# Fused passes over t on DVE, one-hots from a distance, and two gathers in one run

## The chip, the cores and the metric

One core of a Trainium2 chip runs the whole program. The metric is the device time of one execution in microseconds, the median of several runs. TensorE (PE) multiplies, VectorE (DVE) and GpSimd (Pool) work elementwise, ScalarE (ACT) applies functions and copies, SyncE (SP) issues the weight loads. Profiles name the five engines by these short names.

## The reference, cut to what matters

The program computes one step of a two-layer network on 384 tokens (128 context, 256 latent) of width 1024. Each layer is a token mixer and then a mixture of experts:

```
x = layer_norm(ALPHA * x + g1 * mix, ln1_g, ln1_b)          # r is the sum, normalised later
t = x * (1 + sc2) + sh2                                      # what the experts see
group  = argmax(t @ rg_w + rg_b)                             # 1 of 4 groups
top_v, top_i = top_k(t @ re_w + re_b  within the group, 2)   # 2 of its 8 experts
gate   = softmax(top_v) * softmax(group logits)[group]
y      = sum over the two experts e of gate_e * (silu(t @ w1_e) * (t @ w3_e)) @ w2_e
x = layer_norm(ALPHA * x + g2 * y, ln2_g, ln2_b)
```

The reference multiplies every token with all 32 experts and weights by the gate. The kernel computes only the two experts of each token: it sorts the 768 pairs (token, expert) by expert, gathers the rows of t in that order, and runs the experts on windows of 32 rows.

## The kernel before, in words

Tokens lie in NT = 3 tiles of 128. The last column block of the output projection and everything up to the routing is in `last_col` (L983). Per tile i it multiplies (`prod`), adds the residual and takes statistics (`ln1_part`, `ln1_tile`; the reciprocal root is made by Pool, L115 and L116), and transposes r for the logits. `t` of a tile is made in two passes over 1024 columns, `(r - mean) * gain` and `* rstd + bias`. Tile 0 has both fused on DVE (L1022, L1030). Tiles 1 and 2 are normalised by ACT and then multiplied and shifted by Pool (L1003, L1006), tile 2's shift by DVE. For products at nearly full precision t is split in two rounded parts, `thi` (ACT) and `tlo` = t - thi (L1012).

`route` (L1098) masks the expert logits of other groups, takes the two largest, makes one-hot rows `E` of the expert numbers, and counts with matmuls against a triangle of ones how many pairs lie before each (`pc`, a PSUM bank). From that follows `pos`, for each token the two places of its pairs among 768. Three one-hot matrices per block J of 256 places (`onehot`, L1287) are made by DVE with two comparisons of the row numbers 0..255 against the two places of a token, the second adding to the first. A gather is then 48 matmuls of 256 columns: for 8 blocks of 128 rows of t, 3 tiles and the parts thi and tlo, `t^T @ onehot`. `gather0` (L1336) takes tile after tile into four banks; `gather(1)` and `gather(2)` (L1321) take bank after bank, two tags with two buffers each, and each needs its one-hots, which have three buffers. The evacuations write `xT`, transposed rows in expert order.

`second` (L1167) works out which experts have more than CAP = 32 rows and the registers `who`, `more` and `first`; `gates` the softmaxes; `slots` (L1227) builds one-hots of ranks (`RO`) and values (`V`) and multiplies them (12 matmuls, L1252) into the destinations and gates of each row. `windows(q)` copies six windows of 32 rows of xT for quad q by register. `up` (L1377) multiplies a window with quarter kq of the weights of a quad of four experts; `copies` (L1366) copies the weights of experts with an additional window; `down` multiplies with w2, and `scatter` writes the rows to `y_d` in device memory. A weight tile is 1 MB; `done` frees one and lets SP load a later one.

Order: inside `manual_schedule` the engines named there keep the order of the text. In `last_col` that holds for DVE, Pool, ACT and PE, in `experts` before the change for PE alone; DVE, ACT and Pool are ordered there by a planner that simulates the engines, and it may also put instructions of later code into gaps of an ordered part. `issue_after` adds one dependency. The pool `lp` of `last_col` is closed before `experts`, and the pool `ep` (xT, hv, ys) lies over its memory; a tile waits until the tiles under it are no longer used. PSUM has eight banks: tags tp, sc, mm and ms, two each.

Of the kernel before, what the change touches and what calls it, by code (L numbers as in the profile page):

```python
# [8 lines left out]
F32 = mybir.dt.float32  # L9
# [11 lines left out]
D = 1024  # L21
# [56 lines left out]
class Kern:  # L78
# [795 lines left out]
    def open_ln1(self, l):  # L874
# [5 lines left out]
        self.mo = self.ohp = P("mo", bufs=1)  # L880
# [102 lines left out]
    def last_col(self, l, w0, w1):  # L983
# [12 lines left out]
        def norm(i):  # L996
            self.act(t[i], self.r[:, i, :], AF.Identity, scale=self.rs1[:, i:i + 1], bias=self.nm1[:, i:i + 1])

        def nmul(i):
            G.tensor_tensor(self.nm1[:, i:i + 1], self.nmean[:, i:i + 1], self.rs1[:, i:i + 1], op=ALU.mult)  # L1000

        def gain(eng, i, z=slice(0, D)):
            eng.tensor_tensor(t[i][:, z], t[i][:, z], rows["sc20"][:, z], op=ALU.mult)  # L1003

        def bias(eng, i, z=slice(0, D)):
            eng.tensor_tensor(t[i][:, z], t[i][:, z], rows["sh20"][:, z], op=ALU.add)  # L1006

        def hi(i, z=slice(0, D)):
            self.act(self.thi[:, i, z], t[i][:, z], AF.Copy)

        def lo(eng, i, z=slice(0, D)):
            eng.tensor_tensor(self.tlo[:, i, z], t[i][:, z], self.thi[:, i, z].bitcast(F32), op=ALU.subtract)  # L1012

        with self.tc.manual_schedule(engines={e.engine for e in (V, G, nc.scalar, nc.tensor)}):
# [7 lines left out]
            V.scalar_tensor_tensor(t[0], self.r[:, 0, :], self.nmean[:, 0:1], rows["sc21"], op0=ALU.add, op1=ALU.mult)  # L1022
            prod(1, 1)
            self.logit_mm(3, 0)
            self.ln1_part(l, 3, ts, 1)
            self.ln1_tile(l, 1)
            nmul(1)
            prod(2, 0)
            self.logit_tr(3, 1, ts)
            V.scalar_tensor_tensor(t[0], t[0], self.rs1[:, 0:1], rows["sh21"], op0=ALU.mult, op1=ALU.add)  # L1030
            t[1] = lp()
            norm(1)
            gain(G, 1, slice(0, 512))
# [21 lines left out]
            nmul(2)  # L1055
            gain(G, 1, slice(512, D))
# [11 lines left out]
            for z in (slice(0, 512), slice(512, D)):  # L1068
                bias(V, 2, z)
                hi(2, z)  # L1070
            for z in (slice(0, 512), slice(512, D)):
                lo(V, 2, z)
            for i in range(NT):
                G.dma_start(self.t_d[i * 128:(i + 1) * 128, :], t[i])

# [22 lines left out]
    def route(self, l, el):  # L1098
# [40 lines left out]
        self.warm(3)  # L1139
        pr = lpt("pr", (NT, 2, NE))  # L1140
# [4 lines left out]
        self.pos_ins = nc.vector.tensor_reduce(pos.rearrange("p i c -> p (i c)"), pr.rearrange("p i c e -> p (i c) e"), axis=AX.X, op=ALU.add)  # L1145
        self.pc, self.m8, self.e8 = pc, m8, e8

# [19 lines left out]
    def second(self):  # L1167
# [4 lines left out]
        self.posj = S("posj", (2, N6))  # L1172
        for J in range(2):
            V.tensor_scalar(self.posj[:, J, :], pos, -256.0 * (J + 1), None, op0=ALU.add)
        cnt = self.pc[:, 96:128].rearrange("p (q e) -> p q e", e=4)
# [14 lines left out]
        V.tensor_copy(tb[:, 1], self.pc[:, 128:160])  # L1190
# [27 lines left out]
        self.first = S("first", (NE,), I32)  # L1218
        V.tensor_copy(self.first, tb[:, 1])
# [67 lines left out]
    def onehot(self, J):  # L1287

        nc = self.nc
        iota = self.con[:, C_I256:C_I256 + 256]  # L1290
        sj = self.posj[:, J - 1, :] if J else self.place.rearrange("p i c -> p (i c)")
        out = []
        for i in range(NT):
            oh = self.ohp.tile([128, 256], F32R, tag="oh", name="oh", bufs=3)
            nc.vector.tensor_scalar(oh, iota, sj[:, 2 * i:2 * i + 1], None, op0=ALU.is_equal)
            self.oh_ins = nc.vector.scalar_tensor_tensor(oh, iota, sj[:, 2 * i + 1:2 * i + 2], oh.bitcast(F32),
                                                         op0=ALU.is_equal, op1=ALU.add)
            out.append(oh)
        if J == 0:
            self.oh0_ins = self.oh_ins  # L1300
        return out


    def experts(self, l):
# [16 lines left out]
        def gather(J):  # L1321

            oh = self.onehot(J)
            for z in range(4):
                ps = self.bank(("tp", "sc")[z % 2])
                for d2 in range(2):
                    d = z * 2 + d2
                    n = 0
                    for i in range(NT):
                        for t in (self.thi, self.tlo):  # L1330
                            nc.tensor.matmul(ps[:, d2 * 256:(d2 + 1) * 256], t[:, i, d * 128:(d + 1) * 128], oh[i],
                                             start=n == 0, stop=n == 5)
                            n += 1
                evac(J, z, ps)

        def gather0(oh):  # L1336

            ps = [self.bank(("tp", "sc")[z % 2]) for z in range(4)]
# [5 lines left out]
            for n, (i, t) in enumerate(((0, self.thi), (1, self.thi), (0, self.tlo), (1, self.tlo))):  # L1344
                mm(i, t, range(8), n == 0, False)
# [566 lines left out]
```

## Time and profile before

| | us |
|---|---|
| median of 3 runs | 1156.14 (1154.74 to 1159.78) |
| the profiled execution | 1157.68 |
| its span | 1155.8 |
| PE busy | 1026.5 (89%) |
| DVE busy | 822.6 (71%) |
| ACT busy | 414.1 (36%) |
| Pool busy | 288.5 (25%) |
| HBM traffic | 248 GB/s over the span |

The span runs from the first to the last instruction of the profiled execution. A row of a timeline gives the start, the duration, the engine, the line, the operation, the tile written and read, the shape and, in brackets, how long the engine was idle before it and what released it. Consecutive instructions of one kind stand in one row with their count. A line number such as L100 can be that of a helper (L100 is every ACT operation).

### The profile page before, as it was taken

The numbers are of one execution on the slowest core, as the hardware profiler recorded it, in microseconds if no ns is written. First come the engines' busy times: TensorE is split into PE (matmuls) and PEld (weight loads), VectorE is DVE, ScalarE is ACT, GpSimd is POOL, SyncE is SP. The second block draws the span as 40 slices with busy tenths as digits, with TensorE's granted clock in tenths as the row PEclk, the third lists the DMA queues.
The fourth block names the chain that finished last, engine by engine and source line by source line (L and its number), as shares of the span: only waits on it lengthen the run. The fifth ranks groups of instructions, "written<-read, shape, count | busy, mean of one in ns | idle before, by whom it ended". The sixth has DMA issues, their size and how long they took to land. (4 is left out here: it accounts for less than half of the span.)

```text
span 1155.8 us, 20809 instructions
## 1 busy us (share of the span) xinstructions
PE 1026.5 (89%) x8182; PEld 849.1 (73%) x8182; DVE 822.6 (71%) x1530; ACT 414.1 (36%) x739; POOL 288.5 (25%) x246
## 2 busy tenths in 40 slices
PE   7999999999999867966779999999999996887764
PEld 5898968878999856532349897788899996853322
DVE  4389999964457785752479999997744687766338
ACT  4334344443334123422253433444523432233222
POOL 0002411321100550323244043124020055013235
PEclk9999999999999887987989999999999999789787
DMA  9967578357357460999685756764234575279965
GB/s 355 413 241 270 216 253 314 122 184 273 128 203 267 177 237 23 400 420 415 239 346 192 282 202 244 261 254 153 73 112 143 219 274 228 83 273 420 419 260 197
DMA packets 55101, 282.73 MB, mean 245 GB/s; under 512 B 8060, under 2 KB 12284, under 8 KB 27857
## 3 DMA queue, kind: packets, MB, share of 16 engines
q1 hardware_dynamic: 49632, 269.99, 61.2%
q0 software_dynamic: 5360, 11.29, 2.5%
q8 instruction: 69, 1.13, 0.4%
q14 instruction: 40, 0.32, 0.1%
HBM read 262.11 MB, written 24.71 MB: 248 GB/s over the span
## 5 line engine op out<-in xcount | busy, mean ns | idle before, releaser
L95 PE MATMUL ps_mm<-hThi,wr 128*128 128x384 f32 x672 | 229.7, 343 | 5.0 <-ACT hThi L100 2.5
L96 PE MATMUL ps_mm<-hTlo,wr 128*128 128x384 f32 x672 | 227.9, 339 | 0.5 <-DVE hTlo L439 0.4
L108 DVE TENSOR_TENSOR wr<-w_raw,wr 128x1024 fp32r<-128x1024 f32 x124 | 161.8, 1305 | 93.5 <-ACT wr L100 93.3
L97 PE MATMUL ps_mm<-hThi,wr 128*128 128x384 f32 x672 | 227.8, 339 | 0.0
L503 DVE SCALAR_TENSOR_TENSOR cacc<-pad,par,cacc 128x399 f32<-128x399 f32 x240 | 170.1, 709 | 4.2
L100 ACT ACTIVATE wr<-w_raw 128x1024 fp32r<-128x1024 f32 x140 | 147.4, 1055 | 67.4 <-PE ps_mm L97 36.6
L95 PEld LDWEIGHTS ps_mm<-hThi,wr 128*128 128x128 f32 x672 | 127.0, 189 | 19.9 <-ACT hThi L100 4.9
L96 PEld LDWEIGHTS ps_mm<-hTlo,wr 128*128 128x128 f32 x672 | 127.1, 189 | 4.9 <-DVE hTlo L439 2.3
L97 PEld LDWEIGHTS ps_mm<-hThi,wr 128*128 128x128 f32 x672 | 127.2, 189 | 1.8 <-issue 1.0
L1431 POOL DMA_INDIRECT y_d<-ys,dst x28 | 28.6, 1022 | 195.0 <-DVE ys L1446 84.5
L108 POOL TENSOR_TENSOR wr<-w_raw,wr 128x1024 fp32r<-128x1024 f32 x10 | 24.3, 2433 | 200.6 <-ACT wr L100 200.2
L1419 PE MATMUL ps_sc<-w,hidT 128*32 128x512 f32 x256 | 42.6, 750 | 35.7 <-ACT ys L100 24.7
L1389 PE MATMUL ps_mm<-hv,win 128*32 128x128 f32 x1024 | 45.4, 285 | 6.7 <-DVE hv L1374 6.5
L1389 PEld LDWEIGHTS ps_mm<-hv,win 128*32 128x32 f32 x1024 | 33.4, 116 | 24.3 <-DVE hv L1374 13.8
L1383 PE MATMUL ps_mm<-w_raw,win 128*32 128x256 f32 x640 | 50.6, 438 | 0.0
L1374 DVE COPY hv<-w_raw 128x512 f32 x60 | 36.5, 644 | 19.6 <-PE ps_mm L1389 12.0
L100 ACT ACTIVATE gate<-ps_mm 128x384 f32<-128x384 f32 x40 | 19.6, 491 | 84.7 <-PE ps_mm L97 83.6
L217 PE MATMUL ps_ms<-w_raw,cT 128*32 128x512 f32 x320 | 47.7, 624 | 0.0
L1419 PEld LDWEIGHTS ps_sc<-w,hidT 128*32 128x32 f32 x256 | 8.2, 121 | 52.9 <-ACT ys L100 36.8
L909 POOL TENSOR_TENSOR rtmp<-sc,lb 128x1024 f32<-128x1024 f32 x4 | 9.9, 2491 | 122.2 <-DMA lb<-in_ln 122.2
L840 POOL TENSOR_TENSOR merged<-merged,gate 128x384 f32<-128x384 f32 x16 | 18.1, 1138 | 84.8 <-DVE gate L839 84.8
L100 ACT ACTIVATE win<-xT 128x256 f32 x64 | 21.5, 410 | 49.0 <-PE ps_mm L1383 47.6
(497 smaller groups left out, 2450.0 us busy)
## 6 DMA issues: line engine op xcount, KB each, us to landing
w_raw<-in_wst SPq DMA_DIRECT2D x68, 1024.0 KB, 6.3
w_raw<-in_wada SPq DMA_DIRECT2D x48, 1024.0 KB, 5.1
w_raw<-in_w SPq DMA_DIRECT2D x40, 1024.0 KB, 9.7
w<-in_w SPq DMA_DIRECT2D x32, 1024.0 KB, 18.9
w_x<-in_w SPq DMA_DIRECT2D x24, 1024.0 KB, 16.6
bias<-in_bias SPq DMA_DIRECT2D x8, 768.0 KB, 7.4
y_d<-zero SPq DMA_DIRECT2D x2, 3072.0 KB, 14.6
yy<-y_d SPq DMA_DIRECT2D x6, 1024.0 KB, 7.0
```

Source lines behind the costliest of these rows:

```text
L95: mm(out, whi, xhi, start=first, stop=False)
L96: mm(out, whi, xlo, start=False, stop=False)
L97: mm(out, wlo, xhi, start=False, stop=last)
L100: return self.nc.scalar.activation(out, in_, f, **k)
L108: (eng or self.nc.vector).tensor_tensor(lo, x, hi.bitcast(F32), op=ALU.subtract)
L217: nc.tensor.matmul(ps[32 * t:32 * t + 32, :], self.cT[:, 2 * kp + k, :], w[:, t * 512:t * 512 + 512], start=(kp == 0 and k == 0), stop=(kp ...
L503: nc.vector.scalar_tensor_tensor(acc, pad[:, j:j + W], w, acc, op0=ALU.mult, op1=ALU.add)
L1374: nc.vector.tensor_copy(hv[:, i, :], src)
L1383: nc.tensor.matmul(ps[e * 32:(e + 1) * 32, 0:256], x[:, k, e * 32:(e + 1) * 32], w[:, e, kk, :], start=k == 0, stop=k == 7, skip_group_che ...
L1389: nc.tensor.matmul(ps[t * 32:(t + 1) * 32, 256:384], x[:, k, 128 + i * 32:160 + i * 32], hv[:, i, kk, h * 128:(h + 1) * 128], start=False, ...
L1419: nc.tensor.matmul(po[e * 32:(e + 1) * 32, :], hT[:, e * 32:(e + 1) * 32], w2[:, e, :], start=True, stop=True)
L1431: ins = nc.gpsimd.indirect_dma_start(out=view, out_offset=bass.IndirectOffsetOnAxis(ap=dst, axis=0), in_=rows, in_offset=None, bounds_chec ...
```

## The change

In `last_col` the helpers for Pool and ACT go; `mean(i)` and `bias(i)` do both passes on DVE for all three tiles, each one fused instruction. The helper's order of the text changes with it: bias(0) stands ahead of the second tile's residual, mean(1) behind the second tile's statistics, bias(1) inside `route` behind the counting matmuls, mean(2) and bias(2) behind the one-hots of tiles 0 and 1. The gather's matmuls of blocks J = 0 and J = 1 move into `last_col` and run tile by tile, part by part, into eight banks. `route` also works out for each token `mid` = -(p0 + p1) - 512 * (-J), and `dist` = |p0 - p1|; a one-hot is then |2 * iota + mid| (ACT, AF.Abs) compared with dist (DVE). The counts are copied out of `pc` early. In `experts` the rest of the start is written in a fixed order for DVE, ACT and PE: one-hots of block 2, evacuation 0, the registers `first`, `second`, evacuation 1, gather 2, evacuation 2, the other registers, the first windows. `gates` waits for the last window copy, and `slots` stands behind the four products of quad 0.

```diff
-            nmul(1)
+            t[1] = lp()
+            mean(1)
...
-            hi(0)
             t[2] = rows["g11"]
-            norm(2)
-            bias(G, 1)
-            hi(1)
-            lo(G, 0)
-            gain(G, 2)
+            self.thilo(0, t, hi=True)
             self.warm(4)
-            self.route(l, self.logit[:, :, 8:40])
-            self.oh0 = self.onehot(0)
-            lo(V, 1)
...
+            self.route(l, self.logit[:, :, 8:40], lambda: bias(1))
+            hots(0)
+            self.counts()
+            hots(1)
+            self.thilo(1, t, hi)
+            self.gps = {}
+            for i in range(2):
+                self.gather_mm(oh, (0, 1), i, hi)
+            self.thilo(0, t, lo)
+            self.thilo(1, t, lo)
+            for i in range(2):
+                self.gather_mm(oh, (0, 1), i, lo)
+            mean(2)
+            bias(2)
+            hots(2)
+            self.thilo(2, t, hi)
+            self.thilo(2, t, lo)
             for i in range(NT):
                 G.dma_start(self.t_d[i * 128:(i + 1) * 128, :], t[i])
+            for part in (hi, lo):
+                self.gather_mm(oh, (0, 1), 2, part)
...
+    def gather_mm(self, oh, Js, i, part):
+        t = self.thi if part else self.tlo
+        first, last = (i, part) == (0, True), (i, part) == (2, False)
+        for J in Js:
+            for d in range(8):
+                if first and d % 2 == 0:
+                    self.gps[J, d // 2] = self.bank((("tp", "sc"), ("mm", "ms"))[J % 2][d // 2 % 2])
+                self.nc.tensor.matmul(self.gps[J, d // 2][:, d % 2 * 256:(d % 2 + 1) * 256], t[:, i, d * 128:(d + 1) * 128], oh[J, i],
+                                      start=first and d % 2 == 0, stop=last and d % 2 == 1, skip_group_check=True)
...
+        self.act(far, iota, AF.Abs, scale=2.0, bias=self.mid[:, J, i:i + 1])
+        self.nc.vector.tensor_scalar(oh, far, self.dist[:, i:i + 1], None, op0=ALU.is_equal)
...
-        with tc.manual_schedule(engines={nc.tensor.engine}):
-            gather0(self.oh0)
-            with tc.issue_after(self.oh0_ins.ins):
-                self.second()
-            gather(1)
-            gather(2)
+        with tc.manual_schedule(engines={e.engine for e in (nc.vector, nc.scalar, nc.tensor)}):
+            for i in range(NT):
+                self.onehot(oh[2, i], far[:, i, :], 2, i)
+            evacs(0)
+            first = regs(self.first[0:1], [nc.scalar.engine], 2 * T, ...)
+            self.second()
+            evacs(1)
+            for i in range(NT):
+                for part in (True, False):
+                    self.gather_mm(oh, (2,), i, part)
+            evacs(2)
...
+            x = windows(0)
+        with tc.manual_schedule(engines={nc.tensor.engine}):
+            with tc.issue_after(self.win_ins.ins):
+                self.gates(self.logit)
...
+                if q == 0:
+                    self.slots()
```

## Rows read from the trace of the kernel before

**Rows 1.** The page, part 2: GB/s in 40 equal slices.

```profile
GB/s 355 413 241 270 216 253 314 122 184 273 128 203 267 177 237 23 400 420 415 239 346 192 282 202 244 261 254 153 73 112 143 219 274 228 83 273 420 419 260 197
```

**Rows 2.** Stages: us, busy PE, PEld, DVE, ACT, POOL, PEclk, DMA share, GB/s.

```profile
443.00:452.00 9.00, 7.66 (x48) 7.35 (x48) 4.17 (x14) 2.60 (x5) 0.00 (x0) 0.81 0.01 2
452.00:457.50 5.50, 2.77 (x16) 2.68 (x20) 1.99 (x10) 2.79 (x9) 0.00 (x0) 0.75 0.00 0
...
470.00:490.00 20.00, 18.66 (x350) 10.69 (x346) 17.07 (x29) 8.65 (x20) 9.16 (x6) 1.00 1.01 413
```

**Rows 3.** The same table, the weight stream of layer 0.

```profile
462.00:553.00 91.00, 71.09 (x1139) 37.01 (x1132) 46.92 (x93) 28.45 (x62) 28.95 (x20) 0.85 1.01 410
```

**Rows 4.** Timeline of SP's queue: the first load of the stage.

```profile
459.44 8.04 SPq L330 DMA_DIRECT2D w_raw<-in_w  x6
```

**Rows 5.** Timeline of PE, layer 0, gathers to first expert product.

```profile
425.31 0.99 PE L1341 MATMUL ps_tp<-oh,thi 128*128 128x256 f32 x2
...
426.52 0.63 PE L1341 MATMUL ps_tp<-oh,thi 128*128 128x256 f32 x2
426.95 0.63 PE L1341 MATMUL ps_sc<-oh,thi 128*128 128x256 f32 x2
...
428.13 0.40 PE L1341 MATMUL ps_sc<-oh,thi 128*128 128x256 f32 x2
428.37 0.40 PE L1341 MATMUL ps_tp<-oh,tlo 128*128 128x256 f32 x2
...
451.06 0.28 PE L1331 MATMUL ps_sc<-oh,tlo 128*128 128x256 f32 x1
...
457.44 1.94 PE L1383 MATMUL ps_mm<-w_raw,win 128*32 128x256 f32 x16
```

**Rows 6.** Timeline of DVE, layer 0, from the first tile's mean to the windows.

```profile
403.59 1.28 DVE L1022 SCALAR_TENSOR_TENSOR t<-r,nmean,sc 128x1024 f32<-128x1024 f32 x1
405.79 0.42 DVE L944 TENSOR_TENSOR r<-ps_tp,g 128x256 f32<-128x256 f32 x1 [0.91 <-PE ps_tp L488]
...
411.18 1.17 DVE L1089 SCALAR_TENSOR_TENSOR logits<-logits,rs,S 128x40 f32<-128x40 f32 x2
...
413.74 0.77 DVE L1153 TENSOR_TENSOR ex<-logits,m 128x12 f32<-128x12 f32 x1
...
414.62 2.39 DVE L1110 SCALAR_TENSOR_TENSOR em<-pen,logits 128x96 f32<-128x96 f32 x1
...
417.83 1.41 DVE L1154 TENSOR_TENSOR ex<-e 128x6 f32<-128x6 f32 x1
...
419.54 2.28 DVE L1122 TENSOR_TENSOR Eb<-E 128x96 bf16<-128x96 f32 x1
...
422.12 0.26 DVE L1127 TENSOR_TENSOR Eb<-below 128x96 bf16<-128x96 f32 x1
423.16 0.36 DVE L1141 TENSOR_TENSOR pr<-ps_ms,E 128x192 f32<-128x192 f32 x1 [0.78 <-PE ps_ms L1132]
...
423.94 0.35 DVE L1295 TENSOR_SCALAR oh<-con,pos 128x256 fp32r<-128x256 f32 x1
424.33 0.48 DVE L1296 SCALAR_TENSOR_TENSOR oh<-con,pos,oh 128x256 fp32r<-128x256 f32 x1
...
438.10 0.76 DVE L1374 COPY hv<-w_raw 128x512 f32 x2 [1.13 <-issue]
...
451.37 0.69 DVE L1319 COPY xT<-ps_sc 128x512 f32<-128x512 f32 x1 [0.21 <-PE ps_sc L1331]
```

**Rows 7.** Timeline of Pool, layer 0: a reciprocal root and a pass over t.

```profile
403.70 1.61 POOL L116 TENSOR_TENSOR rs<-rs,mhalf 128x1 f32<-128x1 f32 x1
...
414.56 2.34 POOL L1006 TENSOR_TENSOR t<-t,sh 128x1024 f32<-128x1024 f32 x1
```

**Rows 8.** Timeline of ACT, layer 0: a table load.

```profile
450.69 1.28 ACT L100 ACT_TABLE_LOAD   x1
```

**Rows 9.** Timeline of PE, layer 1: the first expert product.

```profile
1016.72 1.94 PE L1383 MATMUL ps_mm<-w_raw,win 128*32 128x256 f32 x16
```

More of the change, by code (lines that the diff above doesn't have):

```diff
@@ L994, in prod, with mean, bias @@
             self.mm_ts((w0, w1)[h], h, ts, self.mhi, self.mlo, (i,))
[L996 to L1012, printed above, removed]
+        def mean(i):
+            V.scalar_tensor_tensor(t[i], self.r[:, i, :], self.nmean[:, i:i + 1], rows["sc20" if i else "sc21"], op0=ALU.add, op1=ALU.mult)
+        def bias(i):
+            V.scalar_tensor_tensor(t[i], t[i], self.rs1[:, i:i + 1], rows["sh20" if i else "sh21"], op0=ALU.mult, op1=ALU.add)
         with self.tc.manual_schedule(engines={e.engine for e in (V, G, nc.scalar, nc.tensor)}):
@@ L1071, in last_col, with hots @@
-            for z in (slice(0, 512), slice(512, D)):
-                lo(V, 2, z)
+            self.thilo(0, t, hi=True)
+            self.warm(4)
+            self.route(l, self.logit[:, :, 8:40], lambda: bias(1))
+            hi, lo = True, False
+            oh = {}
+            def hots(i):
+                for J in range(2):
+                    oh[J, i] = self.lp.tile([128, 256], F32R, tag="oh", name="oh", bufs=6)
+                    self.onehot(oh[J, i], self.lp.tile([128, 256], F32, tag="far", name="far", bufs=2), J, i)
@@ L1139, in route @@
         self.warm(3)
+        between()
         pr = lpt("pr", (NT, 2, NE))
@@ L1285, in slots, with onehot @@
         nc.vector.scalar_tensor_tensor(self.dst[:, 1, :], val[:, 1, :], 2.0, zc.to_broadcast([128, NQUAD]), op0=ALU.mult, op1=ALU.add)
-    def onehot(self, J):
-        nc = self.nc
+    def onehot(self, oh, far, J, i):
         iota = self.con[:, C_I256:C_I256 + 256]
[L1291 to L1301, printed above, removed]
+        self.act(far, iota, AF.Abs, scale=2.0, bias=self.mid[:, J, i:i + 1])
+        self.nc.vector.tensor_scalar(oh, far, self.dist[:, i:i + 1], None, op0=ALU.is_equal)
     def experts(self, l):
@@ L1319, in evac, with evacs @@
                 nc.vector.tensor_copy(o, i_)
-        def gather(J):
-            oh = self.onehot(J)
+        def evacs(J):
             for z in range(4):
[L1325 to L1338, printed above, removed]
-            def mm(i, t, ds, first, last):
-                for d in ds:
-                    nc.tensor.matmul(ps[d // 2][:, d % 2 * 256:(d % 2 + 1) * 256], t[:, i, d * 128:(d + 1) * 128], oh[i],
-                                     start=first and d % 2 == 0, stop=last and d % 2 == 1, skip_group_check=True)
-            for n, (i, t) in enumerate(((0, self.thi), (1, self.thi), (0, self.tlo), (1, self.tlo))):
-                mm(i, t, range(8), n == 0, False)
-            mm(2, self.thi, range(8), False, False)
-            mm(2, self.tlo, range(8), False, True)
-            for z in range(4):
-                evac(0, z, ps[z])
+                evac(J, z, self.gps[J, z])
         def windows(q):
```

55 lines of the change are left out of this document (31 added, 24 removed).

## The prediction

> **What bounds the kernel now.** I read the page's 40 slices first, looking for slices in which the DMA queues move little. Three of them stay under 100 GB/s: 23 at 433 to 462 us, 73 at 809 to 838, 83 at 982 to 1011 [rows 1]. The first and the third lie just ahead of the two expert stages, the slices with 400 and more. The table by stage places the first: from 443 to 457.5 the DMA share is 0.01 and then 0.00, although all 8 quads of expert weights still have to be streamed, and from 462 to 553 the share is 1.01 at 410 GB/s with TensorE's busy time at 71 of 91 us [rows 2, 3]. So the expert stage is paced by its weight stream, and the stream stands still ahead of it, because every buffer is full until the first expert product frees one: the queue issues the next weight load at 459.44 us, 2.0 us after the first product of the expert stage starts at 457.44 [rows 4, 5]. Whatever starts that product earlier moves the stream, and with it the end of the layer, by the same amount. That is the measure for every edit below.
>
> Ahead of the first expert product lies one chain: routing on DVE, one-hots, three gathers on TensorE, evacuations, slot tables, windows. I followed it by the timelines of DVE, Pool and TensorE. The first gather product starts at 425.31, the last at 451.06 [rows 5]. Layer 1 repeats it: its first expert product starts at 1016.72, 559.28 later [rows 9].
>
> **Part 1: routing up to the first gather product.** DVE's timeline shows instructions that are far too long for their size. The one that masks the expert logits (96 columns) takes 2.39 us, and the sum of one-hots Eb (96 columns) 2.28, while an addition of the same 96 columns takes 0.26 two instructions later [rows 6]. The mask runs from 414.62 to 417.01 and Pool's bias pass over t from 414.56 to 416.90 [rows 6, 7]: DVE waits inside the instruction for Pool. The change removes these Pool passes, so I put mask and Eb at 0.28 each, 4.67 becoming 0.56: minus 4.1. The two differences for the gates (0.77 and 1.41, the same stall) leave this stretch, because the gates now come behind the first windows; less what neighbours overlap, minus 2.0. The pair of logit updates at 411.18 takes 1.17 for 40 columns beside a Pool pass; 0.55 is left without it: minus 0.6. Together minus 6.7.
>
> Against that, DVE takes over passes of 1.28 us each [rows 6]. bias(0) moves ahead of the second tile's residual and needs Pool's rsqrt, which itself takes 1.61 us when mean(0) runs beside it and ends at 405.31 [rows 7]; bias(0) then ends at 406.6 where the next DVE work started at 405.79. mean(1) takes the place that bias(0) had. Of the 0.8 us I leave 0.6 on the path, since DVE idled for half a microsecond ahead of the third tile. bias(1) stands where DVE waited 0.78 us for the counts [rows 6] and adds 0.5. Five instructions on three columns make the midpoint and distance: at most 0.26 each by the 96-column addition, 1.3 in all; I take 0.8. The first one-hot took 0.87 us from 423.94 on, in two comparisons; now ACT makes |2 iota + mid| and DVE compares once (0.35). ACT's pass has no row; bounded by DVE's two-input pass over four times the columns, it is below 1.28, and I take 0.45 and 0.1 for the handover: no difference. mean(2) and bias(2) come behind one-hots of tiles 0 and 1, beside 64 matmuls, and cost nothing unless those take under 5 us. Sum of part 1: minus 6.7 + 0.6 + 0.5 + 0.8 = **minus 4.8** (bounds: minus 6.2 if bias(0) and bias(1) find cover entirely and the five cost 0.5; minus 3.5 if they cost 1.3 and ACT's pass 1.28).
>
> Abs is not in the trace before. If ACT had to load a table for it, that would be 1.28 us for a load [rows 8], and one more to come back, on the path: plus 2.6 a layer, the upper end. The Trainium skill (ScalarE: Activation LUTs, Table sets: the hidden batching unit) says that cheap functions such as abs stand in every set. By that rule no load appears and the sum stays; no run so far shows it.
>
> **Part 2: the gathers.** 144 matmuls of 256 columns in both kernels. Now they take from 425.31 to 451.06, 25.75 us start to start. Pairs follow each other at 0.24 us at full clock (428.13, 428.37) and at 0.43 at the start (426.52, 426.95): 0.118 and 0.215 for one [rows 5]. So 143 steps need 16.9 us at full clock; the rest is two waits between the gathers (for the banks, then for the one-hots) and the lower of the two clock levels (1.2 GHz, half speed), into which the engine falls after each wait: the granted clock is 0.81 from 443 to 452 [rows 2]. Afterwards 96 matmuls go into eight banks without a bank wait, with thi and tlo of later tiles made under the earlier ones. The third gather takes its banks from the first gather's four, whose evacuation runs under the second gather's last matmuls and the one-hots already made. I count one stretch of 16 matmuls at the low clock, as rows show after an idle time: plus 1.5. Total 18.4, that is **minus 7.35**. Bounds: everything at full clock, minus 8.9; everything at the low one, 30.7 and so plus 5.0.
>
> The counting bank is now wanted as a gather bank, so TensorE's fourth pair of columns for J=1 waits for counts(), two short DVE copies behind the first one-hots: hidden behind some 14 matmuls. Behind that wait stands the whole gather, which is why it matters that the copy comes ahead of hots(1).
>
> **Part 3: from the last gather product to the first expert product.** Now 6.4 us (451.06 to 457.44): evacuation, gates, windows, the slot tables on DVE and their 12 matmuls. Afterwards the gates wait for the last window copy and the slot tables stand behind quad 0's products. Left are the last matmul (0.3), two evacuations of 0.69 on DVE, the register loads (DVE was idle 1.13 us "issue" ahead of the first copy that uses them), two window copies of half an evacuation's size (0.3 each) and a handover (0.1): 3.5 us, taken as 3.4 because the first evacuations begin before the last product [rows 6]. **Minus 3.0.** The small DVE work of second() now stands in a fixed order ahead of the second evacuation. It is some thirty instructions; at 0.26 each that is 8 us, at half of that, since most have 6 to 32 columns, 4, which I take. The third gather's 48 matmuls last 5.7 us beside it, so it is hidden; at 8 us it would cost about 3: bounds minus 3.0 to 0.
>
> **Sum.** Minus 15.15 a layer, minus 30.3 for two layers. The profiled execution took 1157.68 us (span 1155.8 and 1.9 around it): 1127.4. It lies 1.5 us above the median of the three runs, 1156.14, so by the median 1126. I predict **1127**. The stores of t on Pool's queue no longer stand behind Pool's passes, and on SP's queue no load changes its place. Nothing is given back in the weight stream, if it is as full as before, for it starts earlier and moves the same bytes.
>
> **Rivals.**
>
> 1. *Slot work in front of the stream.* Gates and slot tables now fall into the stage in which DVE copies expert weights by register. DVE was busy 17.07 of 20 us from 470 to 490 [rows 2]. If that work lands ahead of the copies of quad 0, buffers come free later. For: some 9 us of short instructions move there. Against: four freed buffers of 1 MB feed the queue for about 10 us at 410 GB/s, longer than the 5 to 6 us of quad 0. Price: 5 to 9 us a layer, so 1137 to 1145.
>
> 2. *The clock stays low in the gather.* For: TensorE is nearly idle before it in both kernels. Against: rows show the pitch falling to half within 3 us of continuous work. Price: 12.3 us a layer; 15.15 shrinks to 2.9, so 1152.
>
> 3. *The stream loses its density (slower).* In the expert stage DVE is shared by copies, slot work and Pool's affine passes, which stall DVE as in part 1. If the order planned for DVE leaves the products late again and again, the queue runs dry in each quad. The place is the 91 us after the first load; the price is 91 divided by the mean DMA share, minus 91. It eats the 15.15 us when the share falls below 0.86; slower by 0.5% (2.9 us more a layer) from 0.83: 1163 to 1170. For: DVE's load from 470 to 490 and its longer list. Against: the share was 1.01 in that very window [rows 2] and DVE is idle for half of the time later.
>
> 4. *The two gathers do not run together,* because a bank or a tile shared with an earlier user is late (the one-hots of the third gather lie in the buffers of the weight copies, over memory that the gather still reads). Then up to 5 us of the 7.35 goes: 1137. This is the upper end of the forecast's own range.
>
> **Chances.** Forecast 0.70 (own range 1118 to 1137, rival 4 included), better than that 0.03, rival 1 0.14, rival 2 0.06, rival 3 0.07. From 1117 to 1144 holds the forecast and most of rival 1, a little over 8 in 10. A change under 0.5% (5.8 us) cannot be told from none here. Faster: forecast, better, rival 1 and a third of rival 2, 0.89; same: the rest of rival 2, 0.04; slower: rival 3, 0.07.
>
> **What will show it.** Right: DVE's mask and Eb at about 0.3; no Pool pass over t; the first gather product near 420.5 us; 96 gather matmuls without a gap over 0.5 us, their last near 433; the first expert product near 442 and the first weight load behind it near 444, 15 us earlier than now, with DMA share about 1.0 for the following 91 us; about 30 us off the end. Wrong: a table load ahead of Abs; a TensorE gap between the gathers or a granted clock near 0.5 through them (parts 2, rival 2); the first load early but the share of the stream under 0.9 (rivals 1 and 3); or a first expert product that is early while the layer's end is not, which would refute the claim that the stream sets it.

## The result, and the profile after

The changed kernel takes 1128.13 us (median of 4 runs, 1125.47 to 1130.25) against 1157.96 for the kernel before beside it: ratio 0.9743, 95% interval 0.9705 to 0.9781. The prediction was 1127. The profiled execution took 1129.9 us, its span is 1128.1.

The page's slices first, of the kernel after (GB/s in 40 equal slices), to be held against [rows 1]:

```profile
GB/s 359 412 234 257 267 191 315 166 156 277 157 121 226 251 265 127 403 422 410 237 394 181 223 272 224 237 311 124 83 106 136 236 238 193 207 323 421 418 241 204
```

The hole ahead of the first expert stage is still there but less deep, 127 where 23 stood, and the one ahead of the second is 207 where 83 stood. The table by stage (us, busy time of PE, PEld, DVE, ACT, POOL, granted clock, DMA share, GB/s) answers to [rows 2, 3]: the gathers, the third one, the stretch from the last gather product to the first expert product, and the weight stream.

```profile
422.39:434.00 11.61, 11.61 (x96) 11.61 (x97) 9.76 (x18) 5.99 (x11) 0.85 (x2) 1.00 0.63 243
434.00:439.70 5.70, 5.70 (x50) 5.62 (x48) 5.25 (x23) 1.63 (x4) 0.00 (x0) 1.00 0.02 4
439.70:444.40 4.70, 0.13 (x3) 0.00 (x1) 4.53 (x15) 1.65 (x5) 0.00 (x0) 0.86 0.00 0
450.00:541.00 91.00, 69.75 (x1142) 39.12 (x1132) 49.95 (x116) 28.70 (x62) 29.25 (x20) 0.89 1.01 410
```

The stream is as dense as before, 1.01 and 410 GB/s. The gather runs through at granted clock 1.00, that is 2.4 GHz. What is left is the third line: 4.70 us in which TensorE is busy for 0.13 and DVE for 4.53.

TensorE's timeline after (start, us, operation, how many; in brackets the idle time before and what ended it) answers to [rows 5]: first gather product, last of the two gathers, last of the third, first expert product.

```profile
422.39 0.51 PE L1083 MATMUL ps_tp<-oh,thi 128*128 128x256 f32 x2 [1.00 <-DVE oh L1322]
...
433.77 0.40 PE L1083 MATMUL ps_ms<-oh,tlo 128*128 128x256 f32 x2
...
439.43 0.40 PE L1083 MATMUL ps_sc<-oh,tlo 128*128 128x256 f32 x2
444.40 2.42 PE L1378 MATMUL ps_mm<-w_raw,win 128*32 128x256 f32 x14 [4.57 <-ACT win L100]
```

DVE's timeline after, the lines that answer to [rows 6]:

```profile
406.91 1.28 DVE L997 SCALAR_TENSOR_TENSOR t<-r,nmean,sc 128x1024 f32<-128x1024 f32 x1
408.67 1.28 DVE L1000 SCALAR_TENSOR_TENSOR t<-t,rs,sh 128x1024 f32<-128x1024 f32 x1 [0.47 <-POOL rs L116]
...
414.75 0.42 DVE L1107 SCALAR_TENSOR_TENSOR logits<-logits,rs,S 128x40 f32<-128x40 f32 x2
...
416.89 0.26 DVE L1128 SCALAR_TENSOR_TENSOR em<-pen,logits 128x96 f32<-128x96 f32 x1
...
418.47 0.26 DVE L1140 TENSOR_TENSOR Eb<-E 128x96 bf16<-128x96 f32 x1
...
433.98 0.17 DVE L1209 TENSOR_SCALAR full<-cnt 128x32 f32<-128x32 f32 x1
...
436.89 0.35 DVE L1272 TENSOR_TENSOR V<-E,con 128x192 fp32r<-128x192 f32 x1
...
437.31 0.95 DVE L1264 TENSOR_TENSOR RO<-con,rank 128x768 fp32r<-128x768 f32 x1
...
438.86 1.02 DVE L1268 TENSOR_TENSOR RO<-con,sB 128x384 fp32r<-128x384 f32 x2
...
441.34 1.28 DVE L1340 COPY xT<-ps_ms 128x512 f32<-128x512 f32 x2
442.54 1.28 DVE L1340 COPY xT<-ps_sc 128x512 f32<-128x512 f32 x2
443.73 1.09 DVE L1369 COPY hv<-w_raw 128x512 f32 x3
```

The mask em takes 0.26 where it took 2.39, Eb 0.26 where it took 2.28. The queue's next weight load, which stood at 459.44 [rows 4], in layer 0 and layer 1 after:

```profile
447.28 9.89 SPq L330 DMA_DIRECT2D w_raw<-in_w  x6
...
991.38 9.21 SPq L330 DMA_DIRECT2D w_raw<-in_w  x6
```

Where the profiled layers start shifts by some us from one execution to the next (the first tile's mean stood between 401.6 and 406.9 us over all kernels, although no edit lies ahead of it in layer 0). So from here on the stage is measured from that mean: 403.59 us before [rows 6], 406.91 after. All times in us, layer 0 / layer 1:

| from the first tile's mean to | before | after |
|---|---|---|
| first gather product | 21.72 / 21.73 | 15.48 / 15.49 |
| last gather product | 47.47 / 48.04 | 32.64 / 32.64 |
| first expert product | 53.85 / 54.16 | 37.49 / 37.49 |
| weight load behind it | 55.85 / 56.16 | 40.37 / 40.36 |
| that load to the end of the layer | 108.65 / 106.26 | 108.54 / 106.97 |

The two profiled executions differ by 27.7 us of span: +3.3 up to layer 0's mean, minus 15.5 in its stage, minus 0.1 in its stream, +0.7 to layer 1's mean, minus 15.8, +0.7, and minus 1.1 behind the layers (27.8 by rounding).

### The profile page after: what moved, and what is told of

It is laid out like the page before. It is cut to its first block, busy times and chain, and to the rows that moved or that the text cites. A ratio compares the mean times of both kernels' runs of the same rounds, so it can differ in the third digit from the quotient of the medians.

```text
span 1128.1 us, 20783 instructions
## 1 busy us (share of the span) xinstructions
PE 1015.3 (90%) x8182; PEld 845.4 (75%) x8182; DVE 813.4 (72%) x1524; ACT 416.2 (37%) x751; POOL 270.8 (24%) x232
## 4 chain that ended last, share of the span: by engine, by line
PE 26%; DMA 12%; DVE 9%; issue 3%; POOL 3%; ACT 1%; DVEq 0%; SPq 0%; ACTq 0%; POOLq 0%
PE ps_mm L95 6%; PE ps_mm L96 5%; PE ps_mm L97 5%; DMA w<-in_w 4%; DMA y_d<-ys,dst 3%; DMA w_raw<-in_w 2%; DVE cacc L503 2%; DMA w_x<-in_w 2%; PE ps_ms L217 1%; PE ps_mm L1378 1%; DVE wr L108 1%; DMA yy<-y_d 1%; POOL r L1540 1%; DMA w_raw<-in_wada 1%; POOL x L1727 1%
## 5 line engine op out<-in xcount | busy, mean ns | idle before, releaser
L108 DVE TENSOR_TENSOR wr<-w_raw,wr 128x1024 fp32r<-128x1024 f32 x124 | 164.9, 1330 | 96.1 <-ACT wr L100 95.8
L1378 PE MATMUL ps_mm<-w_raw,win 128*32 128x256 f32 x640 | 53.0, 424 | 9.1 <-ACT win L100 9.1
L1384 PE MATMUL ps_mm<-hv,win 128*32 128x128 f32 x1024 | 50.2, 287 | 6.1 <-DVE hv L1369 6.0
L1384 PEld LDWEIGHTS ps_mm<-hv,win 128*32 128x32 f32 x1024 | 38.5, 116 | 20.6 <-DVE hv L1369 11.0
L1378 PEld LDWEIGHTS ps_mm<-w_raw,win 128*32 128x32 f32 x640 | 26.6, 122 | 20.6 <-ACT win L100 10.1
```

The lines of the kernel that those rows point to most:

```text
L108: (eng or self.nc.vector).tensor_tensor(lo, x, hi.bitcast(F32), op=ALU.subtract)
L1378: nc.tensor.matmul(ps[e * 32:(e + 1) * 32, 0:256], x[:, k, e * 32:(e + 1) * 32], w[:, e, kk, :], start=k == 0, stop=k == 7, skip_group_che ...
L1384: nc.tensor.matmul(ps[t * 32:(t + 1) * 32, 256:384], x[:, k, 128 + i * 32:160 + i * 32], hv[:, i, kk, h * 128:(h + 1) * 128], start=False, ...
```

## The experiments

The theory going in: the stage's start moves the stream one for one; part 1 comes from Pool passes that no longer hold DVE; part 2 from running two gathers together; part 3 stayed small because slot-table work entered DVE's list. The first four kernels ran on one chip together; part 1 alone, the split gathers, Pool's reads and DVE's one-hots on another; part 1 alone once more, the memsets and the idle products last. "The base" is the first of them; where a kernel ran apart from it, the ratios to the kernel before are what can be compared.

**The changed kernel again**, in five rounds, as the base for the others.

> The changed kernel once more, on the chip on which the next three run, so that they can be compared with it. Theory (the weight stream of the expert stage is moved as a whole): again 0.974 of the kernel before, within 0.004, and in each layer about 15.5 us less from the start of the last column block to the first weight load of the expert stage, while that load stays 106 to 109 us ahead of the loads of the expert outputs. Rival (part of the gain is a lucky order of transfers in one execution): ratio above 0.98.

1130.04 us, ratio 0.9771 (0.9748 to 0.9794). First weight load 40.97 / 40.39 us from the mean. The stage repeats itself to 0.6 us; it is the sharper measure for what follows.

**Does the stream follow its start?** Five ACT copies ahead of the first windows; nothing reads them.

```diff
+            for _ in range(5):
+                self.act(win[:, 1].rearrange("p k c -> p (k c)")[:, 0:D], self.r[:, 0, :], AF.Copy)
             x = windows(0)
```

> The changed kernel with five idle copies of 1024 columns on ScalarE ahead of the first windows of each layer (they write a buffer that is overwritten later; nothing is left out). One such pass has a step of 0.95 us in the trace, so the first expert product comes some 4.7 us later in each layer. Theory (the stream follows the first expert product one for one): 9.4 us slower than the changed kernel, ratio to the kernel before 0.982 to 0.983. Rival 1 (the stream has slack that takes up a late start): under 4 us slower, ratio under 0.978. Rival 2 (a late start also thins the stream): more than 14 us, ratio above 0.986.

1134.2 us, ratio 0.9803 (0.9774 to 0.9831): 4.2 us over the base, with some 4 us of uncertainty by the two intervals, less than expected. ACT's timeline of this kernel shows why the delay itself is less than five copies: the first runs at a time at which ACT would have waited for DVE's evacuations anyway.

```profile
438.00 1.06 ACT L100 ACTIVATE win<-r 128x1024 f32<-128x1024 f32 x1 [1.78 <-DVE most L1254]
...
439.48 3.22 ACT L100 ACTIVATE win<-r 128x1024 f32<-128x1024 f32 x3
...
442.73 1.06 ACT L100 ACTIVATE win<-r 128x1024 f32<-128x1024 f32 x1
```

The first expert product came 3.3 and 4.8 us later, the load 3.3 and 4.7, and the stream kept its length (108.21 / 107.30). Together the loads come 8.1 us later, while the profiled pair differs by 3.7: of the other 4.4 us, 1.7 lay ahead of layer 0's mean, 1.3 between the layers and 1.4 in the two streams, 1.2 of it in layer 1's, whose length is 107.0 and 108.5 in the two executions of the changed kernel itself. So the stream's start follows the first product, and its end follows within that spread; by total time the theory is only not refuted.

**Slot tables out of the way.** Their issue waits for the last window copy.

```diff
                 if q == 0:
-                    self.slots()
+                    with tc.issue_after(self.win_ins.ins):
+                        self.slots()
```

> The changed kernel with one added dependency: the slot tables wait for the last copy of the first windows. In the changed kernel VectorE makes four of their instructions (0.35, 0.95 and 2 in 1.02 us) inside the stretch between the first and the second evacuation. Theory (after the last gather product VectorE's list is what the first expert product waits for): the first product comes 2.2 us earlier in each layer, 4.4 us in all, ratio to the kernel before about 0.970. Rival (TensorE and ScalarE set it, VectorE only seems late): under 1 us, ratio 0.974.

1124.71 us, ratio 0.9723 (0.97 to 0.9746), 5.3 under the base. First expert product 36.29 / 36.20, against 38.11 / 37.50: 1.8 and 1.3 us earlier. Four instructions of V and RO in DVE's list were indeed on the path.

**Evacuations first.** As the last, and DVE's count work straight behind the third one-hots, the first two gathers evacuated by ACT alone, the registers for the weight copies loaded behind the first windows.

```diff
-            evacs(0)
+            self.second()
+            evacs(0, False)
             first = regs(self.first[0:1], [nc.scalar.engine], 2 * T, "a place among all rows, worked out as one")
-            self.second()
-            evacs(1)
+            evacs(1, False)
...
-            who = regs(self.who[0:1, 0:2 * NQUAD], [nc.vector.engine, nc.scalar.engine], 3, "a place among four, worked out as one")
...
             x = windows(0)
+            who = regs(self.who[0:1, 0:2 * NQUAD], [nc.vector.engine, nc.scalar.engine], 3, "a place among four, worked out as one")
```

> As the run with late slot tables, and also: ScalarE alone evacuates the first two gathers, the work on counts starts on VectorE as soon as the third gather's one-hots are made, and the registers of the weight copies are loaded behind the first windows. Then nothing but two evacuations, a register load and the window copies stands between the last gather product and the first expert product. Theory: that gap shrinks from 4.85 to about 2 us, in each layer 2.8 to 3.3 us earlier, 6 us in all, ratio about 0.969. Rival (the evacuations on one engine hold up the third gather's banks by more than the half microsecond that I count): no better than the run with late slot tables.

1122.79 us, ratio 0.9698 (0.9664 to 0.9731): the fastest kernel of the study, below the changed one by 7.3 us. From the last gather product to the first expert product it takes 1.72 / 1.71 us (4.85 in the changed kernel), and the load stands at 38.02 / 36.79. TensorE's and DVE's timelines of this kernel:

```profile
436.68 0.40 PE L1083 MATMUL ps_sc<-oh,tlo 128*128 128x256 f32 x2
438.52 1.99 PE L1378 MATMUL ps_mm<-w_raw,win 128*32 128x256 f32 x16 [1.44 <-ACT win L100]
```

```profile
436.64 1.29 DVE L1340 COPY xT<-ps_sc 128x512 f32<-128x512 f32 x2 [1.24 <-PE ps_sc L1083]
...
440.63 1.10 DVE L1369 COPY hv<-w_raw 128x512 f32 x3 [1.12 <-issue]
441.64 0.95 DVE L1264 TENSOR_TENSOR RO<-con,rank 128x768 fp32r<-128x768 f32 x1
```

DVE now waits for TensorE ahead of the last evacuation (1.24 us), and RO stands behind the first copies of weights. The stages give 2.95 and 3.6 us, 6.55 of the 7.3. The six runs lay in two groups, 1114.1 and 1116.1 against 1121.5 to 1125.8; what parts them is open. The profile shown is one of the first group: its span is 14.1 us shorter than the base's, and 7.5 of these lie outside the stages (3.7 between the layers, 2.9 in the two streams). By total time this version and the one before it can't be told apart; by its first expert product it is 1.2 and 1.8 us ahead.

**Part 1 alone** on the kernel before: the fused passes, without the new one-hots and without the common gather.

```diff
+        def mean(i):
+            V.scalar_tensor_tensor(t[i], self.r[:, i, :], self.nmean[:, i:i + 1], rows["sc20" if i else "sc21"], op0=ALU.add, op1=ALU.mult)
...
+        def bias(i):
+            V.scalar_tensor_tensor(t[i], t[i], self.rs1[:, i:i + 1], rows["sh20" if i else "sh21"], op0=ALU.mult, op1=ALU.add)
...
-            norm(2)
-            bias(G, 1)
-            hi(1)
-            lo(G, 0)
-            gain(G, 2)
```

> The kernel before with part 1 alone: both passes over t of all three tiles are fused on VectorE in the places of the changed kernel (bias(1) inside the routing), Pool does no pass over t; one-hots, gathers, evacuations, slot tables and the planner's freedom stay as before. Theory (VectorE was held inside its routing instructions by Pool's passes): the mask and the sum Eb take under 0.35 us each, the first gather product comes 15.5 to 16 us after the start of the first tile's mean instead of 21.7; VectorE then makes tlo of tile 0 and all of tile 2 later than Pool did, which gives back about 2 us in the first gather; first expert product at +49 to +50 instead of 53.9, ratio to the kernel before 0.991 to 0.994. Rival (VectorE's own passes take as much as Pool's stalls did): first gather product above +19, ratio above 0.997.

1157.01 us in ten runs, ratio 1.0006 (0.9992 to 1.002): nothing. The first gather product came at 15.29 / 15.29 us, 6.4 earlier than before. But the gathers, 25.75 and 26.3 us before, then took 30.9 and 28.4. TensorE's timeline, its gaps, and the table by stage (columns as above):

```profile
424.41 0.50 PE L1328 MATMUL ps_tp<-oh,thi 128*128 128x256 f32 x2 [2.62 <-ACT thi L100]
...
431.85 0.58 PE L1318 MATMUL ps_tp<-oh,thi 128*128 128x256 f32 x1 [2.92 <-DVE oh L1283]
```

```profile
425.00:434.00 9.00, 6.04 (x28) 5.35 (x27) 8.57 (x33) 1.75 (x4) 0.31 (x1) 0.69 0.14 54
```

The gather reached the third tile's thi and the next one-hots before they were made, and the granted clock was 0.69 over these 9 us. DVE is busy for 8.57 of them: it now makes tlo of tile 0, which Pool had made, and two whole passes over tile 2 instead of one. The weight load stood at 53.86 / 52.10, so 2.0 and 4.1 us of the 6.4 were left in the stages. The profiled run is the fastest of the ten, 4.3 us under their median.

**Part 1 alone once more**, since a stage gain of 6 us beside a ratio of 1.0006 was not understood.

> The kernel before with part 1 alone, a second look. Its first profile showed the first weight load of the expert stage 2.0 and 4.1 us earlier than in the kernel before, and lay 4.3 us under the median of its own ten timings, which showed no gain (1.0006 of before). Theory: the serial gathers give back most of part 1, a varying share by how long the clock stays low in them, so the load comes 0 to 4 us earlier in either layer. Rival (the gain of the first profile is steady and is lost later in the kernel): again 2 and 4 us earlier, with the layer's rest longer.

One run, 1159.26 us. The load came at 53.88 / 52.77, 2.0 and 3.4 us earlier than before: that gain is steady. What is given back lies outside the stages: 1.1 us in the first profile, 7.1 in this one (2.9 ahead of layer 0's mean, 2.2 between the layers, 3.0 in the two streams, minus 1.0 behind the layers). Over all kernels the stretch between the layers varies from 392.1 to 397.3 us (394.5 before, 397.3 and 396.7 here) and layer 1's stream from 106.2 to 108.9, so two profiles don't show that part 1 lengthens them. Why ten runs show no gain is open.

**The gathers one after the other**: the changed kernel, with J = 1's 48 products behind all of J = 0's.

```diff
-                self.gather_mm(oh, (0, 1), i, hi)
+                self.gather_mm(oh, (0,), i, hi)
...
+            for i in range(NT):
+                for part in (hi, lo):
+                    self.gather_mm(oh, (1,), i, part)
```

> The changed kernel with the 48 matmuls of block 1 all behind the 48 of block 0, in the same eight banks. Theory: block 0 alone does not cover the making of tile 2, so TensorE waits about 3.5 us for it and the second gather ends 3.5 us later; the third gather too, but VectorE's list behind the first evacuation hides part of it, and the first expert product comes 1.5 to 2.5 us later in each layer, ratio to the kernel before 0.980. Rival (the whole gain of the gathers, 8.6 us a layer, comes from running the two together): 8 us a layer later, ratio 0.991.

1134.39 us, ratio 0.9805 (0.9783 to 0.9828). The last gather product came at 37.51 / 36.63 us, 4.3 and 4.0 later than in the base; at the third tile TensorE stood for 2.18 us until ACT had made its thi. The first expert product came only 2.8 and 2.6 later, because DVE's list was waiting there in any case. Running together is worth some 4 us of the gather, and a good half of that at the end.

**Pool reads beside the route**: the changed kernel with four additional Pool products of two rows, which nothing reads.

```diff
+            dum = self.lp.tile([128, D], F32, tag="dum", name="dum")
+            for _ in range(4):
+                G.tensor_tensor(dum, rows["lg"], rows["lb"], op=ALU.mult)
             self.thilo(0, t, hi=True)
```

> The changed kernel with four idle Pool passes (1024 columns, two inputs, 2.35 us each, into a tile that nobody reads) behind the last reciprocal root, so that they run beside the routing as Pool's passes did before; nothing is left out. Theory (VectorE instructions with two inputs in memory wait inside the instruction for a Pool instruction that reads): mask and Eb above 2 us each again, first gather product 4 to 7 us later in each layer, 8 to 14 us in all, ratio to the kernel before 0.984 to 0.989. Rival (the gain of part 1 is that work left the routing's dependencies, not the Pool stall): under 1 us a layer, ratio 0.977.

1143.4 us, ratio 0.9888 (0.9856 to 0.992). Pool's and DVE's timelines of this kernel:

```profile
412.23 9.70 POOL L1044 TENSOR_TENSOR dum<-lg,lb 128x1024 f32<-128x1024 f32 x4
```

```profile
412.57 2.05 DVE L1110 SCALAR_TENSOR_TENSOR logits<-logits,rs,S 128x40 f32<-128x40 f32 x1
414.66 0.17 DVE L1113 MAX8 m<-logits 128x8 f32<-128x8 f32 x1
...
415.14 1.88 DVE L1128 TENSOR_TENSOR pen<-con,i 128x12 f32<-128x12 f32 x1
417.05 0.26 DVE L1131 SCALAR_TENSOR_TENSOR em<-pen,logits 128x96 f32<-128x96 f32 x1
...
418.24 1.48 DVE L1140 TENSOR_TENSOR E<-con,j 128x192 f32<-128x192 f32 x1
419.75 2.29 DVE L1143 TENSOR_TENSOR Eb<-E 128x96 bf16<-128x96 f32 x1
```

Each of the four passes holds one two-input instruction until it ends: Eb again takes what it took before (2.29 against 2.28 [rows 6]), a penalty of 12 columns takes 1.88. The one-input MAX8 between them takes 0.17. The mask em is not hit this time; it started 0.02 us ahead of the third pass. Less what the four take undisturbed (0.26, 0.17, 0.36 and 0.26 in the changed kernel), the holds add up to 6.65 us. The first gather product came 6.6 us later, so the holds are the whole delay, and none of it is work that queued up behind Pool. The first expert product came 6.7 and 7.6 us later. That is as much as part 1 had gained, taken back by Pool alone.

**Pool writes beside the route**: ten memsets in the place of the four products, as long a stretch (10.15 us).

```diff
+            dum = self.lp.tile([128, D], F32, tag="dum", name="dum")
+            for _ in range(10):
+                G.memset(dum, 0.0)
```

> As the run with four idle Pool passes, but with ten Pool fills of the same unread tile instead (they write memory and read none). Theory: VectorE is held only by a Pool instruction that reads; logit updates, mask, E and Eb stay under 0.5 us and the first gather product at +15.5 from the first mean, while Pool is busy through the routing. Rival (any Pool instruction on the memory holds VectorE): two-input instructions of VectorE last as long as a fill again, first gather product later than +17.

One run, 1136.01 us. Pool's and DVE's timelines:

```profile
412.96 10.15 POOL L1044 MEMSET dum<- 128x1024 f32 x10
```

```profile
414.30 0.26 DVE L1131 SCALAR_TENSOR_TENSOR em<-pen,logits 128x96 f32<-128x96 f32 x1
...
415.88 0.26 DVE L1143 TENSOR_TENSOR Eb<-E 128x96 bf16<-128x96 f32 x1
...
419.39 1.77 DVE L1325 TENSOR_SCALAR oh<-far,dist 128x256 fp32r<-128x256 f32 x2 [0.30 <-ACT far L100]
...
421.42 1.84 DVE L1325 TENSOR_SCALAR oh<-far,dist 128x256 fp32r<-128x256 f32 x2
```

The routing is untouched, and the first gather product comes at 15.87 us. So it is not any work of Pool's that stalled the routing before; passes that read did (two inputs each; one with a single input was not tried). But the pairs of one-hots, of one input, took 1.77 and 1.84 us instead of 0.75 and 0.67, and the last gather product came 3.9 and 5.8 us later, Pool's own late stores being part of that (one evacuation of DVE's waits 3.92 us for them). The slow one-hots were not expected. The Trainium skill (SBUF — State Buffer, Who interferes with whom) says that a DVE instruction with two inputs contends only with Pool work that reads, and that copy, cast and tensor_scalar can, under conditions on their operands, enter forms that use the port pair shared with Pool, and contend with it then. Both runs agree with it: 0.26 beside memsets and 2.29 beside reads for Eb, 1.8 for two tensor_scalar comparisons beside memsets.

**One-hots by two DVE comparisons**, as before, in the changed kernel.

```diff
...
-        self.act(far, iota, AF.Abs, scale=2.0, bias=self.mid[:, J, i:i + 1])
-        self.nc.vector.tensor_scalar(oh, far, self.dist[:, i:i + 1], None, op0=ALU.is_equal)
+        sj = self.posj[:, J, :]
+        self.nc.vector.tensor_scalar(oh, iota, sj[:, 2 * i:2 * i + 1], None, op0=ALU.is_equal)
+        self.nc.vector.scalar_tensor_tensor(oh, iota, sj[:, 2 * i + 1:2 * i + 2], oh.bitcast(F32), op0=ALU.is_equal, op1=ALU.add)
```

> The changed kernel with the one-hots made as before, by two comparisons on VectorE (the second adds to the first), with three shifted copies of the places instead of midpoint and distance. Theory: the first gather product comes within 0.4 us of the changed kernel's; VectorE has 9 times half a microsecond more, so tile 2 is about 1.5 us late for the gather and the first expert product about 2.5 us later in each layer, ratio to the kernel before 0.981. Rival (one-hots are off the path, ScalarE's help is worth nothing): within 0.5 us a layer.

1131.97 us, ratio 0.9785 (0.9762 to 0.9809); the base stood at 0.9771, so the totals don't tell them apart. In the stage the first gather product is unmoved (15.53 / 15.74), the last 0.9 and 1.7 later, the first expert product 1.4 and 2.2. ACT's form is worth DVE's time during the gather, not a shorter way to its start.

**Without the idle products** that TensorE runs during the routing.

```diff
-            self.warm(4)
...
-        self.warm(3)
```

> The changed kernel without the idle matmuls that stand ahead of and inside the routing (8 and 6 in the trace; their products are read by nobody). In the changed kernel the granted clock was 1.00 through the first two gathers. Theory: the short routing lets these matmuls hold the high clock level; without them the first gather starts at the low level, its first 16 to 30 matmuls take 0.21 us instead of 0.12, and the last gather product comes 1.5 to 3 us later; VectorE's list hides part of it, 2 to 4 us in all, ratio to the kernel before about 0.980. Rival (the clock is kept by the projection that ends ahead of the routing): no change in the gather's pitch.

1132.29 us, ratio 0.9794 (0.9765 to 0.9822). TensorE's timeline and the table by stage of this kernel:

```profile
418.21 0.77 PE L1082 MATMUL ps_tp<-oh,thi 128*128 128x256 f32 x2 [2.44 <-DVE oh L1320]
...
421.68 0.40 PE L1082 MATMUL ps_tp<-oh,thi 128*128 128x256 f32 x2
```

```profile
418.21:421.70 3.49, 3.49 (x17) 3.49 (x18) 3.46 (x8) 2.54 (x5) 0.00 (x0) 0.52 0.81 329
421.70:437.00 15.30, 15.30 (x130) 15.18 (x128) 11.51 (x32) 5.02 (x10) 0.85 (x2) 1.00 0.28 103
```

Some 16 products go at half speed (granted clock 0.52, the 1.2 GHz level), and the gather ends 0.9 and 1.4 us later. The total does not show it. In the changed kernel the idle products end 1.00 us ahead of the gather, and no product of it runs slowly.

## Why the prediction was right

The sum was right, 15.15 us a layer against 15.5 and 15.8, out of terms that were not. In the order of its steps:

- **What bounds the kernel.** Right. The stream kept its share (1.01) and its length, and its start moved with the first expert product: shown by the two kernels and by the added delay.
- **Part 1, minus 4.8: measured minus 6.2,** its lower bound. The stalls went as priced: by the starts of the rows, mask and Eb give minus 4.15 (4.1 in the step), the differences for the gates minus 2.0 (2.0), the pair of logit updates minus 0.75 (0.6). What was off is the new work. bias(0) and mean(1) cost 0.25 where 0.6 stood, bias(1) 0.3 where 0.5 stood, and from the first instruction behind pos to the first gather product 1.37 us (423.94 to 425.31 [rows 5, 6]) became 1.21 (421.18 to 422.39), where the step had added 0.8. The one-hot itself does take 0.3 longer. But in the kernel before it was done at 424.81 [rows 6], and the first gather product came 0.5 us later, straight behind six idle products; in the changed kernel it comes right behind its one-hot. TensorE's rows in the kernel before (the last two are for part 2):

```profile
421.87 0.18 PE L1132 MATMUL ps_ms<-Eb,tri 128*128 128x32 bf16 x1 [8.14 <-DVE Eb L1122]
...
422.96 2.91 PE L1080 MATMUL ps_mm<-con 128*128 128x256 f32 x6
...
434.81 0.58 PE L1331 MATMUL ps_tp<-oh,thi 128*128 128x256 f32 x1 [2.13 <-ACT xT L100]
...
443.68 0.36 PE L1331 MATMUL ps_tp<-oh,thi 128*128 128x256 f32 x1 [1.66 <-DVE oh L1296]
```

  That the stalls are Pool's reads was shown by putting reads back (+6.6) and writes (nothing in the routing).
- **No table load for Abs.** Right: 7 loads on ACT in both kernels. By the rule that the prediction quoted from the Trainium skill (ScalarE: Activation LUTs, Table sets: the hidden batching unit) no load was to come, and the trace agrees.
- **Part 2, minus 7.35: measured minus 8.6 and minus 9.2,** about the lower bound of minus 8.9. The 1.5 us for a stretch at the low clock did not come. The step took the clock of the gather's start from the kernel before. There the idle products end only where the gather starts (422.96 above), but TensorE had stood for 8.14 us ahead of the counts. In the changed kernel idle products and counts follow each other from 415.33 to 421.39 with gaps under 0.4 us, and then 1.00 us is idle. Taking the idle products out brought back 16 products at half speed, as the step had priced. Some 4 us of the gain is the two gathers running together, as the split gathers show. The rest goes with the two waits of the kernel before that are gone, 2.13 us for banks and 1.66 for one-hots (the last two rows above), and the slow products behind them; these were not tried apart.
- **Part 3, minus 3.0: measured minus 1.5 and minus 1.3.** Here the step failed: "the slot tables stand behind quad 0's products" holds for TensorE's part alone. Their DVE instructions waited for nothing, and the list set V and the three of RO between those of second(), 436.89 to 439.8. With them second() took from 433.98 to 441.34, 7.4 us where 4 were taken and 8 were the upper bound, and the second gather's evacuation (441.34) and the third's (442.54) came behind. Less the four slot instructions, some 3.0 us from start to start, second() took 4.4: its own size was right. Issuing the slots later gave 1.8 and 1.3 us back; ordering the rest, 3.1 in all.
- **A term that was missing:** from the first expert product to the load behind it, 2.0 us became 2.9. The load waits for the last of the 16 products that read its tile, which ends at 447.25. In the kernel before, ACT had copied the four windows of quad 0 some 3 us ahead, and the first products on them started within 0.02 us of each other. In the changed kernel TensorE starts on the first window while ACT copies the others, one each 0.31 us, and the first product on the fourth comes 0.94 us behind that on the first. The prediction had carried the 2.0 us over, without a price for windows that are still being copied. The register copies of these weights, which now stand beside the windows (443.73), are not the cause: they were done 0.1 us after the first product here, and in the run with the delay 3.7 us before it, and the load came 2.9 us behind it both times. ACT's timeline before and after, and what the queue waits for last ahead of 447.28:

```profile
452.89 2.60 ACT L100 ACTIVATE win<-xT 128x256 f32 x8 [0.70 <-DVE se L1162]
```

```profile
443.93 2.61 ACT L100 ACTIVATE win<-xT 128x256 f32 x8 [1.11 <-DVE xT L1340]
```

```profile
SPq L330 <- PE ps_mm L1378: 2.7, 1, 2.7
```

In layer 0 minus 6.24, minus 8.59, minus 1.53 and plus 0.88 are minus 15.48: parts 1 and 2 gained 2.7 us more than stood in the sum, part 3 and the release 2.35 less. That the two nearly cancel is luck.

The rivals: slot work in front of the stream did come, but what it cost lay inside part 3, ahead of the first product: 1.3 to 1.8 us a layer instead of 5 to 9. The gates and the rest of the slot work do stand among quad 0's copies on DVE (446.7 to 449.1), and the stream kept its share. The clock was not low, the stream lost nothing, and the gathers ran together.

One thing the prediction did not see: its terms don't add. Part 1 alone gives no time (1.0006), and the changed kernel with as much taken back by Pool gives 0.9888, yet together they give 0.9771. In the stages part 1 alone kept 2.0 and 4.1 of its 6.4 us: the gathers, one after the other, came earlier to a thi and to one-hots that DVE, with more to make, did not have ready. The common gather is not all that lets the earlier start through, for the split gathers still give 0.9805; what the eight banks, ACT's one-hots and the new order do for it was not tried apart.

## What to carry to other kernels

Price a two-input DVE instruction by what Pool reads beside it, not by its columns, and look for the same operation without such company to see what is left. When an order says that work stands behind something, ask on which engine: the part without a wait on the others goes wherever the planner finds a hole, even into the chain that ends last. Before adding the gains of two edits of one chain, ask whether the stage between them can take an earlier start.

## What was not expected of the hardware

One-input comparisons on DVE were held by Pool's memsets (a pair 1.8 us instead of 0.7) while two-input instructions beside them were not (0.26 both ways). And the hold goes both ways: Pool's root of 128 values took 1.61 us beside a DVE pass over t, as before [rows 7], and 0.57 where none ran (in the stages of all kernels, 1.41 to 1.62 beside such a pass and 0.56 or 0.57 without). In the changed kernel the first of these lines is what bias(0) waits 0.47 us for:

```profile
407.02 1.61 POOL L116 TENSOR_TENSOR rs<-rs,mhalf 128x1 f32<-128x1 f32 x1
...
415.04 0.57 POOL L116 TENSOR_TENSOR rs<-rs,mhalf 128x1 f32<-128x1 f32 x1
```
